# Sliding-window queries projected feature-major, in a two-layer hybrid decoder trunk

## The chip, the core and the metric

The kernel runs on one core of a Trainium2 chip. The profile knows five engines of that core: TensorE, shown as PE with its weight loads apart as PEld; VectorE (DVE), ScalarE (ACT), GpSimd (POOL), and SyncE (SP), whose queue issues all the kernel's DMAs. The metric is the time on the device in microseconds, lower is better. A profiled execution is one execution of the same program with the hardware profiler on; its span is the time from the first to the last instruction of the program.

## What is computed

A decoder trunk of two equal layers on 512 tokens of 1024 features, all in float32. One projection of the normalized input feeds two branches:

```python
h = rmsnorm(x, pre_mix_g)
proj = h @ w_in
(dn_q, dn_k, dn_v, dn_z, dn_b, dn_a, sw_q, sw_k, sw_v, gate_a, gate_b) = split(proj)
y_a = deltanet_branch(dn_q, dn_k, dn_v, dn_z, dn_b, dn_a, ...) @ w_up_dn
y_b = swa_sink_branch(sw_q, sw_k, sw_v, positions, sinks) @ w_up_sw
mix = (sigmoid(gate_a) * y_a + sigmoid(gate_b) * y_b) @ w_o
x = x + rmsnorm(mix, post_mix_g)
ff = square(relu(rmsnorm(x, pre_mlp_g) @ w_ff1)) @ w_ff2
x = x + rmsnorm(ff, post_mlp_g)
```

The second branch is what the change touches. It has 16 query heads of 64 features and 2 key/value heads (8 query heads share one), a window of 128 tokens and a learned sink for each head. The first 16 features of every query and key head are rotated: with halves x1 and x2 of 8 features each, `x1*cos - x2*sin` and `x2*cos + x1*sin`, angles by token position. The columns b and a of the projection (8 each) are the write strength and the decay of the first branch.

## The kernel before

**Number format.** Every large product is made from three matmuls: an operand is split into a rounded part (`_h`, a cast on ACT) and a rest (`_l`, a subtraction on DVE), and h·h, h·l and l·h are summed in PSUM. Weights come in pieces of at most 128x1024 (`load`, L265, five buffers `wr`) and are split by `prefetch` (L311: ACT L319, DVE L320) into four buffers each of `wh` and `wl`, so that conversion runs four pieces ahead of use.

**Two layouts.** `mm_a` (L331) takes a 128-column piece of weights as the stationary operand and streams 512 tokens: 24 matmuls of 512 columns, the result is [feature, token]. `mm_a2` (L340) is the same in two halves of 256 tokens. `mm_b` and `mm_b4` (L350, L373) keep 128 tokens stationary and stream weight columns: the result is [token, feature].

**The start of a layer.** The normalized input is transposed tile by tile (128 tokens each; `norm_turn`, L449, matmuls L455 into `ps_n`) into `hT`. The 1296 columns b, a, query, key, value are then projected in [token, feature] by three chunks of 432 columns (`NB`), each of 4 token tiles x 24 matmuls: chunk 0 at L495 to L559, chunks 1 and 2 at L655 to L659. `evac_b` (L590) copies them to `ba`, `qt[t]` (four tiles 128x1024) and `kv[t]`. In the first layer the work up to chunk 0 has an order on PE, ACT, DVE and SP that is written out by hand (`Order`); in the second layer the last tiles of the layer before and chunk 0 are in one such order on PE alone. Between chunk 0 and 1 stand the decay tables: a row `gd` is stored to DRAM, loaded back spread over 128 partitions (L646), masked on POOL (L647), exponentiated on ACT (L649, L651) and stored (`dd`).

**Attention.** Sixteen groups (tile t of 128 queries, key head g, e: even or odd heads of the eight), in the order t, g, e. `att_rope` (L770) rotates queries and keys of a tile on POOL; `att_prep` (L787) makes the values' two parts and transposes the keys (`ps_k`, L801); `att_q` (L810) transposes the queries of (t, g) by four PE transposes into `ps_q` (L814), and ACT L819 and DVE L820 scale and split them. Then a group makes its scores (L846, L847), a softmax on DVE and ACT (L850 to L870), a transpose of the probabilities (`ps_pt`, L876), and the product with the values (L892), written back over the queries in `qt[t]` as [feature, token] (L895, L896). At the end 32 pieces of 128x128 are split into `oT` for the up-projection (L1118 to L1124).

**What fills PE beside it.** `MIX` names for each of the 16 groups the projection units traced ahead of it: K (a DeltaNet key head, with its conv and its triangular matrix stored to DRAM), G and GA (merge gates). After the groups come the DeltaNet projections (`d_dense`), the up-projection, and the head-by-head chain.

**Order.** Everything outside the hand-written orders is placed by a list scheduler at build time: on each engine an instruction goes when its inputs are ready by a planner's model of durations, the earlier traced first. On the chip each queue then runs in that fixed order and waits where the plan was too early. SP's queue is one of those queues.

Of the kernel before, what the change touches and what calls it, by code (L numbers as in the profile page):

```python
# [20 lines left out]
P = 128  # L21
# [16 lines left out]
OFF_B, OFF_GA, OFF_GB = 4096, 5392, 6416  # L38
NB = 432
# [4 lines left out]
XB = 6  # L44

MIX = "G K K G K K G K K G K K G GA GA GA".split()
NA = sum(c.count("A") for c in MIX)
NA2 = NA + 2
LASTK = max(i for i, c in enumerate(MIX) if "K" in c)
PMB = 2  # L50


def chunk_order(depth):
# [3 lines left out]
    for l in range(depth):  # L57
        a_in = lambda w, c: out.append(("chunk", w, l, 0, c, 0))
        b_in = lambda w, r, c, n: out.append(("chunk", w, l, r, c, n))
        for n in range(3):  # L60
            for j in range(4):
                b_in("w_in", j * 256, OFF_B + n * NB, NB)
        n_ = {"K": 0, "G": 0, "A": 0}
        for c in "".join(MIX):
            a_in("w_in", {"K": OFF_K, "G": OFF_GB, "A": OFF_GA}[c] + n_[c] * P)
            n_[c] += 1
# [41 lines left out]
def pack(inputs, depth=2):  # L108

    keys = chunk_keys(depth)  # L110
    out = np.zeros((len(keys), P, 1024), np.float32)
    for i, (name, l, r, c, n) in enumerate(keys):
        k, n = (2, n) if n else (8, P)
        w = np.asarray(inputs[name])[l, r:r + k * P, c:c + n].reshape(k, P, n)
        out[i, :, :k * n] = w.transpose(1, 0, 2).reshape(P, k * n)
    return out
# [3 lines left out]
def hybrid_trunk(ctx, tc, x, positions, pre_mix_g, dn_conv_w, dn_a_log, dn_dt_bias, dn_norm_g,  # L120
# [35 lines left out]
    def X4(name):  # L156
        return up.tile([P, D], F32, name=name, tag="x4", bufs=XB)

# [87 lines left out]


    xd = dr.tile([S, D], F32, name="xd")
    gad = dr.tile([KT, P, 512], F32, name="gad")
# [15 lines left out]
    def load(key):  # L265

        wr = wp.tile([P, 1024], F32, name="wr", bufs=WR)
        w = 2 * key[4] if key[4] else 1024
        dma(wr[:, :w], wpk[index[key], :, :w])
        return wr  # L270

    def blocks(a, n_):
        return a[:, :2 * n_ if n_ else 1024].rearrange("p (k c) -> p k c", k=2 if n_ else 8)

    def seven(w, l, r0):
# [23 lines left out]
        return [(lambda f=f, j=j: f(j), 512) for f in makes for j in range(2)]  # L299
# [3 lines left out]
    for kind_, *key in chunk_order(depth):  # L303
        if kind_ == "seven":
            specs.extend(seven(*key))
        else:
            specs.append((tuple(key), key[4]))
# [3 lines left out]
    def prefetch(n, wr=None, sub=tt):  # L311
        while len(pre) < min(n, len(specs)):
# [5 lines left out]
            w = 2 * n_ if n_ else 1024  # L318
# [31 lines left out]
    def mm_b(ps, ws, aT, t, ks=range(KT)):  # L350
        tsl = slice(t * P, (t + 1) * P)
        for k in ks:
            hi, lo = aT[k]
            wh, wl = ws[k // 2]
            mm(ps, lhsT=hi[:, tsl], rhs=wh[:, k % 2, :], start=k == 0, stop=False)  # L355
            mm(ps, lhsT=hi[:, tsl], rhs=wl[:, k % 2, :], start=False, stop=False)  # L356
            mm(ps, lhsT=lo[:, tsl], rhs=wh[:, k % 2, :], start=False, stop=k == KT - 1)  # L357
# [54 lines left out]
    def gain(g):  # L412
        gb = X4("gb")
# [50 lines left out]
    def post_tile(a0g, ps1, add1, q0, gb, xsrc):  # L464
# [4 lines left out]
        xo = X4("xo")  # L469
# [12 lines left out]
    def pre_begin(l):  # L482
        if l > 0:
            return halves_of(gain(pre_mix_g[l])), *quads("h")

        row = X4("row")
        dma(row[0:1, :], pre_mix_g[l].rearrange("(o d) -> o d", o=1))
# [5 lines left out]
    for l in range(depth):  # L493

        pb0 = [b("ps_b") for b in (PM, PM, PK, PS)]  # L495
        nbs = slice(0, NB)
        if l == 0:
            order = Order(nc.tensor, nc.scalar, nc.vector, nc.sync)
            order.begin()
            xts = [X4("x0") for t in range(NT)]  # L500
# [10 lines left out]
            part = lambda t, j: mm_b(pb0[t][:, nbs], pre, hT, t, range(2 * j, 2 * j + 2))  # L511
# [16 lines left out]
            for j in range(2):  # L528
                part(1, j)
            xs.append(scale(2))  # L530
            ps2 = norm_turn(xs[2], 2, qs, 0)
            prefetch(3, wrs[2])
            for t in range(2):
                part(t, 2)
            rs.append(rstd("nr", *q[3]))
            xs.append(scale(3))
            norm_turn(xs[2], 2, qs, 1, ps2)
            ps3 = norm_turn(xs[3], 3, qs, 0)
            prefetch(4, wrs[3])
            for j in range(3):  # L540
                part(2, j)
            for t in range(3):
                part(t, 3)
# [822 lines left out]
```

## Time and profile before

| | |
|---|---|
| median of 3 timed runs | 1876.22 us (1875.23 to 1876.54) |
| profiled execution: time, span | 1874.57 us, 1872.9 us |
| instructions | 26807 |
| DVE, ACT, POOL busy | 68%, 50%, 11% of the span |
| moved by DMA | 255.40 MB, the queue of SP takes 42.0% of the 16 engines' time |

In the profile's rows a matmul row has a start, a modelled duration that overlaps the next one, and in brackets the idle time before it with what ended it. Since matmuls overlap, the cost of one is read from the distance between two starts. Names like `ps_q<-ident,qt` say what is written and read.

### The profile page before, as it was taken

The page shows a single profiled execution, that of the slowest core. Times are in us where ns is not written, and L with a number is a line of the kernel's source. Part 1 is how long each engine was busy: PE and PEld are TensorE (multiplying, and loading weights), DVE is VectorE, ACT ScalarE, POOL GpSimd, SP SyncE. Part 2 cuts the span into 40 slices and gives each one's busy share as a digit, 9 for nine tenths or more (in the row PEclk, how much of TensorE's full clock was granted, in tenths as well). Part 3 has the DMA queues.
Part 4 walks back from the last instruction along what each step waited for, and adds up shares of the span by engine and source line. Part 5 has one row for each costly group of instructions (what it writes and reads, how often), then busy time and mean ns, then how long its engine had stood idle before and what let it go on. Part 6 is the DMA issues. An engine that isn't in the chain of part 4 may idle for free. (4 is left out here: it accounts for less than half of the span.)

```text
span 1872.9 us, 26807 instructions
## 1 busy us (share of the span) xinstructions
PE 1847.6 (99%) x9716; PEld 1534.1 (82%) x9716; DVE 1281.5 (68%) x2466; ACT 939.7 (50%) x1913; POOL 208.1 (11%) x385
## 2 busy tenths in 40 slices
PE   8999999999999999999999999999999999999998
PEld 7888788888888888888888887888888888888886
DVE  5499795777656667684556997857775667586834
ACT  6678732344434645454356887233333346454442
POOL 1322102121100000000012221022111000000000
PEclk9999999999999999999999999999999999999999
DMA  5633436333363253544245333553433533534631
GB/s 179 202 115 117 120 125 196 102 119 109 86 215 127 91 188 97 176 168 170 83 143 188 103 126 105 160 173 102 125 97 110 194 124 99 183 114 158 205 119 45
DMA packets 123445, 255.40 MB, mean 136 GB/s; under 512 B 32609, under 2 KB 49313, under 8 KB 123314
## 3 DMA queue, kind: packets, MB, share of 16 engines
q1 hardware_dynamic: 123314, 253.71, 42.0%
q8 instruction: 76, 1.25, 0.3%
q14 instruction: 55, 0.45, 0.1%
HBM read 224.70 MB, written 28.97 MB: 135 GB/s over the span
## 5 line engine op out<-in xcount | busy, mean ns | idle before, releaser
L320 DVE TENSOR_TENSOR wl<-wr,wh 128x1024 fp32r<-128x1024 f32 (+1 forms) x332 | 402.6, 1222 | 331.2 <-ACT wh L319 323.4
L319 ACT CAST wh<-wr 128x1024 fp32r<-128x1024 f32 (+1 forms) x332 | 344.1, 1041 | 561.8 <-PE ps_f L336 145.9
L335 PE MATMUL ps_f<-g_h,wh 128*128 128x512 f32 x448 | 174.3, 389 | 0.0
L336 PE MATMUL ps_f<-g_l,wh 128*128 128x512 f32 x448 | 174.3, 389 | 0.0
L337 PE MATMUL ps_f<-g_h,wl 128*128 128x512 f32 x448 | 174.3, 389 | 0.0
L397 PE MATMUL ps_p<-wl,P_h 128*128 128x512 f32 x336 | 131.2, 391 | 0.8 <-DVE wl L320 0.8
L399 PE MATMUL ps_p<-wh,P_l 128*128 128x512 f32 x336 | 130.8, 389 | 0.0
L395 PE MATMUL ps_p<-wh,P_h 128*128 128x512 f32 x336 | 129.5, 389 | 0.0
L434 POOL TENSOR_TENSOR pr<-pq,pw 128x1 f32<-128x1 f32 x16 | 9.3, 583 | 809.5 <-DVE pq L433 809.5
L336 PEld LDWEIGHTS ps_f<-g_l,wh 128*128 128x128 f32 x448 | 84.1, 188 | 17.5
L335 PEld LDWEIGHTS ps_f<-g_h,wh 128*128 128x128 f32 x448 | 84.1, 188 | 17.4
L337 PEld LDWEIGHTS ps_f<-g_h,wl 128*128 128x128 f32 x448 | 84.1, 188 | 17.4
L397 PEld LDWEIGHTS ps_p<-wl,P_h 128*128 128x128 f32 x336 | 63.1, 188 | 15.6 <-DVE wl L320 2.3
L395 PEld LDWEIGHTS ps_p<-wh,P_h 128*128 128x128 f32 x336 | 63.1, 188 | 13.3 <-ACT wh L319 0.2
L399 PEld LDWEIGHTS ps_p<-wh,P_l 128*128 128x128 f32 x336 | 63.1, 188 | 12.8
L382 PE MATMUL ps_b<-wh,h_h 128*128 128x432 f32 (+1 forms) x192 | 71.1, 371 | 0.0
L383 PE MATMUL ps_b<-wl,h_h 128*128 128x432 f32 (+1 forms) x192 | 70.4, 367 | 0.0
L384 PE MATMUL ps_b<-wh,h_l 128*128 128x432 f32 (+1 forms) x192 | 70.0, 366 | 0.0
L285 DVE TENSOR_TENSOR wr<-wr 128x1024 f32<-128x1024 f32 x48 | 58.0, 1221 | 2.4 <-DMA wr<-in_weights_dram 1.9
L335 PE MATMUL ps_qp<-h_h,wh 128*128 128x512 f32 x128 | 54.9, 429 | 0.0
L336 PE MATMUL ps_qp<-h_l,wh 128*128 128x512 f32 x128 | 54.1, 423 | 0.0
L864 ACT ACTIVATE M<-M,nm 128x128 f32<-128x128 f32 x128 | 49.8, 391 | 5.9 <-DVE nm L859 5.9
(356 smaller groups left out, 4855.4 us busy)
## 6 DMA issues: line engine op xcount, KB each, us to landing
wr<-in_weights_dram SPq DMA_DIRECT2D x308, 512.0 KB
wr<-in_weights_dram SPq DMA_DIRECT2D x24, 432.0 KB
D<-dd SPq DMA_DIRECT2D x32, 256.0 KB
xd<-xo SPq DMA_DIRECT2D x12, 512.0 KB
xt<-xd SPq DMA_DIRECT2D x24, 256.0 KB
D<-gd SPq DMA_DIRECT2D x16, 256.0 KB
dd<-D SPq DMA_DIRECT2D x16, 256.0 KB
kkd<-kk SPq DMA_DIRECT2D x16, 256.0 KB
```

The costliest lines, as they stand in the source:

```text
L285: tt(out=a, in0=a, in1=o, op=ALU.add)
L319: nc.scalar.copy(wh[:, :w], wr[:, :w])
L320: sub(out=wl[:, :w], in0=wr[:, :w], in1=wh[:, :w].bitcast(F32), op=ALU.subtract)
L335: mm(ps, lhsT=wh[:, k, :], rhs=hi, start=k == 0, stop=False)
L336: mm(ps, lhsT=wh[:, k, :], rhs=lo, start=False, stop=False)
L337: mm(ps, lhsT=wl[:, k, :], rhs=hi, start=False, stop=k == KT - 1)
L382: mm(pss[t], lhsT=hi[:, tsl], rhs=wh[:, r, :], start=k == 0, stop=False)
L383: mm(pss[t], lhsT=hi[:, tsl], rhs=wl[:, r, :], start=False, stop=False)
L384: mm(pss[t], lhsT=lo[:, tsl], rhs=wh[:, r, :], start=False, stop=k == KT - 1)
L395: mm(pss[t], lhsT=hi[:, c], rhs=wh[:, r, :], start=first, stop=False, skip_group_check=onto)
L397: mm(pss[t], lhsT=hi[:, c], rhs=wl[:, r, :], start=False, stop=False, skip_group_check=onto)
L399: mm(pss[t], lhsT=lo[:, c], rhs=wh[:, r, :], start=False, stop=last, skip_group_check=onto)
```

## The change

Only keys, values, b and a stay in [token, feature]: `NB` becomes 272, and the weights of these columns are packed in three pieces of three, three and two 128-row blocks (`w_bkv`, `rows_of`). The queries become eight units of `mm_a`, called `q_unit`, whose result stands in two tiles `q8[g]` of 128x2048 as [feature, token]; unit 0 is made in the hand-written order by `mm_a2`. Four units are traced before the attention, four among its first three groups (`MIX`).

Rotation of the queries now goes through DRAM and DVE: `q_rope` stores the rows to be rotated from four places of `q8[g]` (8 partitions each), loads them packed into 128 partitions, once as they are and once with the halves exchanged, makes three DVE operations with tables `cosT` and `sinT`, stores the result and loads it back to the four places. The tables are made once in `rotary` (16 ACT copies, 8 PE transposes), which is traced later than before, and loaded in each layer. The transposes of `att_q` fall away: it reads `q8` directly. Groups run in the order (0,0), (1,0), (0,1), (1,1), (2,0), (2,1), (3,0), (3,1) for (t, g), and `att_ready` issues rotation and transposition of keys and the splitting of queries one group ahead; values (`att_values`) are prepared inside the group. The decay tables are traced after the third query unit (`decays`). `X4` buffers of 128x1024 become halves of `X8` buffers of 128x2048, three in all.

```diff
-OFF_B, OFF_GA, OFF_GB = 4096, 5392, 6416
-NB = 432
+OFF_B, OFF_SQ, OFF_SK, OFF_GA, OFF_GB = 4096, 4112, 5136, 5392, 6416
+NB = 272
...
-MIX = "G K K G K K G K K G K K G GA GA GA".split()
+MIX = "QQ KQ QK G KG KG G KG K GK GK G A A A A".split()
 NA = sum(c.count("A") for c in MIX)
-NA2 = NA + 2
+NA2 = NA + 1
+BKV = 0, 3, 6
...
+        for c in range(2):
+            ct = T[6 + c]("ct")
+            cv = ct.rearrange("p (t a b i) -> p t a b i", t=NT, a=2, i=HALF)
+            for a in range(2):
+                for t in range(NT):
+                    src = cs[:, t, c, :].unsqueeze(1).broadcast_to([P, 8, HALF])
+                    act(out=cv[:, t, a], in_=src, func=AF.Copy, scale=-1.0 if c > a else 1.0)
+            ps = PS("ps_cs")
+            for t in range(NT):
+                tr(ps[:, t * P:(t + 1) * P], ct[:, t * P:(t + 1) * P], ident)
+            ctT = T[6 + c]("ctT")
+            nc.scalar.copy(ctT, ps)
+            dma(csd[c], ctT)
...
-            ws = [weights() for _ in range(4)]
-            for t in range(NT):
-                mm_b(pb0[t][:, nbs], ws, hT, t, range(4))
-                if t == 1:
-                    norm_turn(xs_next[2], 2, nxt[1])
-                mm_b(pb0[t][:, nbs], ws, hT, t, range(4, KT))
-                if t == 1:
-                    norm_turn(xs_next[3], 3, nxt[1])
+            ws = [weights() for _ in range(3)]
+            pb0 = [PZ("ps_b"), PZ("ps_b"), None, None]
+            for t in range(2):
+                mm_b(pb0[t][:, :NB], ws, hT, t, rows=3)
+            ps_q0, w_q0 = PM("ps_q"), weights()
+            for j in range(2):
+                mm_a2(ps_q0, hT, 0, w_q0, range(j * 4, j * 4 + 4))
+                norm_turn(xs_next[2 + j], 2 + j, nxt[1])
+            for t in range(2, 4):
+                pb0[t] = (PM, PK)[t - 2]("ps_b")
+                mm_b(pb0[t][:, :NB], ws, hT, t, rows=3)
+            mm_a2(ps_q0, hT, 1, w_q0)
...
+        def q_rope(g):
+            spots = [(q8[g][e * HD + a * HALF:e * HD + (a + 1) * HALF].rearrange("p (m n) -> p m n", m=4),
+                      lambda d, a=a, e=e: d[g, a].rearrange("(m e) i n -> e i m n", e=2)[e])
+                     for e in range(2) for a in range(2)]
+            for a, d in spots:
+                dma(d(qd), a)
+            r_, rs_ = T[2]("rq"), T[3]("rq")
+            flat = lambda d: d.rearrange("a b i n -> (a b i) n")
+            dma(r_, flat(qd[g]))
+            for a in range(2):
+                dma(rs_[a * 64:(a + 1) * 64], qd[g, 1 - a].rearrange("b i n -> (b i) n"))
+            tt(out=r_, in0=r_, in1=tables[0], op=ALU.mult)
+            tt(out=rs_, in0=rs_, in1=tables[1], op=ALU.mult)
+            tt(out=r_, in0=r_, in1=rs_, op=ALU.add)
+            dma(flat(qrd[g]), r_)
+            for a, d in spots:
+                dma(a, d(qrd))
+
+        def q_unit(m):
+            if m == 0:
+                ps = ps_q0
+            else:
+                ps = PM("ps_q")
+                mm_a(ps, hT)
+            nc.scalar.copy(q8[m // 4][:, m % 4 * 512:(m % 4 + 1) * 512], ps)
+            if m % 4 == 3:
+                q_rope(m // 4)
...
         def att_q(t, g):
-            ps = PS("ps_q")
-            for i in range(4):
-                j = g * 4 + i
-                tr(ps[:, i * P:(i + 1) * P], qt[t][:, j * P:(j + 1) * P], ident)
+            q_ = c4(q8[g])[:, :, t * P:(t + 1) * P]
...
+        for m in range(4):
+            q_unit(m)
+            if m == 1 and l == 0:
+                rotary()
+            if m == 2:
+                tables = q_tables()
+                decays()
+        def att_ready(i):
+            if i + 1 < 16 and groups[i + 1][1:] == (0, 0):
+                att_rope(groups[i + 1][0])
+            if i < 16:
+                t, g, e = groups[i]
+                if (g, e) == (0, 0):
+                    att_keys(t)
+                if e == 0:
+                    att_q(t, g)
+        att_rope(0)
+        att_ready(0)
         for i in range(16):
...
             late = g
+            att_ready(i + 1)
             if i > LASTK:
                 steps(3)
...
-        for t in range(NT):
-            tsl = slice(t * P, (t + 1) * P)
-            for g in range(2):
-                for j in range(g * 4, g * 4 + 4):
-                    hi, lo = oT[j]
-                    split(qt[t][:, j * P:(j + 1) * P], hi[:, tsl], lo[:, tsl])
+        for j in range(KT):
+            split(q8[j // 4][:, j % 4 * 512:(j % 4 + 1) * 512], *oT[j])
```

In the first layer the hand-written order at the start changes with it: tile 1 gets three of its eight row blocks ahead of the transposes of tile 2 and not four, `evac_b` of tiles 0 and 1 stands inside that order, and after the transposes of tile 3 the first half of query unit 0 comes ahead of tile 3's projection, the second half behind it.

## What is predicted, and why

> **What bounds the kernel now.** I read the page's busy times first, then busy time by stage, then PE's waits, then PE's own rows.
>
> ```profile
> span 1872.9 us, 26807 instructions
> PE 1847.6 (99%) x9716; PEld 1534.1 (82%) x9716; DVE 1281.5 (68%) x2466; ACT 939.7 (50%) x1913; POOL 208.1 (11%) x385
> core 0: us, PE busy (x) PEld busy (x) DVE busy (x) ACT busy (x) POOL busy (x), PEclk, DMA share, GB/s
> 0.00:76.00 76.00, 68.85 (x335) 62.58 (x336) 36.71 (x92) 49.15 (x111) 15.00 (x36) 1.00 0.66 214
> 76.00:230.00 154.00, 151.26 (x788) 123.59 (x787) 129.00 (x374) 116.72 (x340) 36.38 (x68) 1.00 0.36 112
> 941.00:1004.00 63.00, 60.34 (x315) 56.60 (x314) 31.11 (x65) 38.10 (x91) 12.04 (x21) 1.00 0.58 195
> 1004.00:1158.00 154.00, 151.26 (x789) 123.61 (x788) 128.94 (x375) 116.62 (x340) 36.75 (x70) 1.00 0.36 112
> ```
>
> PE is the bound: of 1872.9 us it lacks 25.3. The four windows are the stages that the change rebuilds, in both layers: the start of a layer (0 to 76, 941 to 1004) and the sixteen attention groups (76 to 230, 1004 to 1158). There PE lacks 7.2, 2.7, 2.7 and 2.7 us, 15.3 together: no better order can give back more than that. What else can be won is work of PE's own. Work of DVE, ACT or POOL counts only where PE waits for it:
>
> ```profile
> PE ps_n L455 <- DVE xs L446: 5.5, 7, 2.2
> PE ps_pt L876 <- ACT M L870: 3.9, 6, 0.8
> ...
> PE ps_g L627 <- DVE lw L625: 1.0, 1, 1.0
> ```
>
> In the attention it waits mainly for the softmax on ACT (3.9 us, six times in both layers); no row says that it waits for queries or keys.
>
> **Step 1: query transposes go.** They are 64 matmuls, in 16 bursts of four.
>
> ```profile
> L814 PE MATMUL ps_q<-ident,qt 128*128 128x128 f32 x64 | 9.6, 272 | 0.0
> 79.88 0.28 PE L801 MATMUL ps_k<-ident,kv 128*128 128x128 f32 x1
> 79.99 0.60 PE L814 MATMUL ps_q<-ident,qt 128*128 128x128 f32 x4
> 80.34 0.48 PE L335 MATMUL ps_kp<-h_h,wh 128*128 128x512 f32 x1
> ...
> 131.64 0.60 PE L814 MATMUL ps_q<-ident,qt 128*128 128x128 f32 x4
> 132.00 0.48 PE L337 MATMUL ps_kp<-h_h,wl 128*128 128x512 f32 x1
> 132.31 0.39 PE L335 MATMUL ps_kp<-h_h,wh 128*128 128x512 f32 x1
> ```
>
> Matmuls overlap, so the cost is the distance between starts: 79.99 to 80.34 and 131.64 to 132.00, 0.355 us a burst, 5.7 for 16. Behind a burst the next matmul takes 0.31 and not 0.23 (step 2): 0.08 more. Half of the bursts belong to groups that transpose keys as well (79.88), which stays, so this counts 8 times: 0.6. **Sum: -6.3 us.** Nothing fills the place, as PE has other units ready in almost all of these 308 us.
>
> **Step 2: the same columns, cut otherwise.** A layer projected 4 x 24 x 3 = 288 matmuls of 432 columns. Now it is 96 of 272, 7 units x 24 of 512, and 48 of 256 (unit 0): 124416 columns in both.
>
> ```profile
> 59.90 0.36 PE L382 MATMUL ps_b<-wh,h_h 128*128 128x432 f32 x1
> ...
> 74.22 0.35 PE L384 MATMUL ps_b<-wh,h_l 128*128 128x432 f32 x1
> 74.41 0.39 PE L335 MATMUL ps_gb<-h_h,wh 128*128 128x512 f32 x1
> ...
> 79.64 0.40 PE L337 MATMUL ps_gb<-h_h,wl 128*128 128x512 f32 x1
> ...
> 600.94 0.28 PE L346 MATMUL ps_f<-g_h,wh 128*128 128x256 f32 x1
> ...
> 608.01 0.28 PE L348 MATMUL ps_f<-g_h,wl 128*128 128x256 f32 x1
> ```
>
> 75, 24 and 60 matmuls from the first to the last of each pair: 14.32/74 = 0.1935 us, 5.23/23 = 0.2274, 7.07/59 = 0.1198. No row has 272 columns; it lies between 0.1198 and 0.1935, and a straight line gives 0.1265. Before 288 x 0.1935 = 55.73 us; after 96 x 0.1265 + 168 x 0.2274 + 48 x 0.1198 = 56.09. **+0.36 a layer, +0.7.** If 272 columns cost no more than 256 it is -0.3 a layer.
>
> **Step 3: tables.** Eight transposes in the first layer, 8 x 0.355/4 and twice 0.08 behind them: **+0.9**. Their 16 ACT copies and the sine now stand behind the second query unit. PE runs a fixed order, so if the plan puts the transposes too early it waits: `ps_g` above, also behind a chain of small ACT and DVE operations, cost 1.0. I take 0 and keep 2 as the upper bound, as three more query units are there to fill.
>
> **Step 4: the two starts.** In the first layer, when the transposes of tile 3 begin, 36 matmuls of 432 are done (7.0 us); now 57 of 272 would be (7.2 us). The weights for the next unit come free earlier, as only the last piece is held to the end. I take 0, between -1 and +1. In the second layer the transposes of tiles 2 and 3 wait for a DVE and ACT chain that the change doesn't touch:
>
> ```profile
> 952.53 0.35 PE L357 MATMUL ps_b<-wh,h_l 128*128 128x432 f32 x1
> 954.61 1.29 PE L455 MATMUL ps_n<-ident,xs 128*128 128x128 f32 x8 [1.73 <-DVE xs L446]
> 955.66 0.44 PE L355 MATMUL ps_b<-wh,h_h 128*128 128x432 f32 x1
> ```
>
> Until 955.66 PE got 48 matmuls of 432 done, 9.3 us of work. Now its order holds 48 of 272 and 24 of 256 ahead of that point, 6.1 + 2.9 = 8.9 us: **+0.3**, and the idle time of 1.73 us grows to some 2.7.
>
> The trace has a second fact for this place. At the start of the kernel, after PE had waited for its input:
>
> ```profile
> 13.72 0.71 PE L355 MATMUL ps_b<-wh,h_h 128*128 128x432 f32 x1
> ...
> 16.02 0.48 PE L355 MATMUL ps_b<-wh,h_h 128*128 128x432 f32 x1
> 16.34 0.36 PE L356 MATMUL ps_b<-wl,h_h 128*128 128x432 f32 x1
> 16.54 0.36 PE L357 MATMUL ps_b<-wh,h_l 128*128 128x432 f32 x1
> ```
>
> From 13.72 to 16.02 lie six distances, 0.38 us on average; from 16.34 on it is 0.20, while the wait of 1.73 us at 954.61 leaves it at 0.19 to 0.20. So a long pause makes PE slow for a while, and a short one doesn't. [...]
>
> **Step 5: rotation by DRAM, the one new wait.** Query unit 3's result goes out by four stores, comes in by three loads, three DVE operations, one store, four loads, and only then ACT and DVE can split the queries of group 0. The nearest chain in the trace is the decay row: stored, and loaded back.
>
> ```profile
> 43.08 0.33 SPq L639 DMA_DIRECT2D gd<-gT  x1
> 43.51 0.37 SPq L642 DMA_DIRECT2D egd<-egT  x1
> 44.50 2.71 SPq L646 DMA_DIRECT2D D<-gd  x6
> ...
> 47.73 0.64 POOL L647 TENSOR_SCALAR_AFFINE_SELECT D<-D 128x512 f32<-128x512 f32 x1 [28.97 <-DMA D<-gd]
> ...
>   POOL D L647: 2.9, 2
> L820 DVE SCALAR_TENSOR_TENSOR qT<-ps_q,qT 64x512 fp32r<-64x512 f32 x32 | 22.0, 689 | 1.8 <-ACT qT L819 0.9
> L819 ACT ACTIVATE qT<-ps_q 64x512 fp32r<-64x512 f32 x32 | 18.9, 591 | 6.8 <-DVE qT L820 5.2 <-PE ps_q L814 1.3
> L595 ACT COPY qt<-ps_b 128x432 f32<-128x432 f32 x8 | 3.7, 510 | 0.0
> ```
>
> A store takes 1.4 us from its issue to that of the load behind it, a load 3.2 to its user, each further issue on SP 2.71/6 = 0.45. The chain: copy 0.5; stores 1.4 + 3 x 0.45 = 2.8; loads 3.2 + 2 x 0.45 = 4.1; DVE 3 x 0.69 = 2.1; store 1.4; loads 3.2 + 1.4 = 4.6; splitting 0.6 + 0.7. That is **16.8 us**. In that time PE has query units 4 and 5, 48 x 0.2274 = 10.9 us, and behind them a K unit of 5.5 us that needs nothing of the chain: 16.4 together. So PE is covered if its fixed order puts the K unit ahead of the first scores, and waits 16.8 - 10.9 = 5.9 us a layer if it does not. Between 0 and 11.8 for both layers; I take 0, since in the decay chain the plan was late for ACT only (2.9 us before L649 in both layers, the row "POOL D L647") and PE lost nothing by it. Queued behind the waiting instructions: on ACT the copies of units 4 and 5 and the weight casts (four converted pieces lie ahead, 4 x 5.5 = 22 us), on DVE the other half of the conversion, on SP the weight loads, which also run at least four pieces ahead. The chain for units 4 to 7 has groups 2 and 3 and more units ahead of its user and is not late.
>
> **Costed at nothing**, since PE doesn't wait for it: POOL's query rotation goes; DVE gains six rotation operations a layer (4.1 us) and loses by splitting `oT` in 8 pieces and not 32, and by the copies of `kv`:
>
> ```profile
> L407 DVE TENSOR_TENSOR oT_l<-qt,oT_h 128x128 fp32r<-128x128 f32 x64 | 16.7, 298 | 4.9 <-ACT qq L665 2.9 <-ACT oT_h L406 1.5 <-PE ps_k L801 0.5
> L598 DVE COPY kv<-ps_b 128x256 f32<-128x256 f32 x8 | 3.3, 416 | 0.0
> ```
>
> That is 32 x 0.30 - 8 x 0.69 + 4 x 0.42 = 5.8 us a layer off DVE, so its 129 us in the attention's 154 don't grow. One gate unit more stands in the attention and one less behind the up-projection: same work of PE.
>
> **The sum:** -6.3 + 0.7 + 0.9 + 0.3 = **-4.4 us**. The profiled execution took 1874.57 (span 1872.9 and 1.7 around it), which would become 1870.2. The median of the runs is 1876.22, 1.65 above it; the same 4.4 off gives **1871.8 us**.
>
> **The rivals.** A measurement of this kernel tells 0.2% (3.75 us) from no change, so 1872.5 and 1880.0 are the limits.
>
> *The rotation isn't covered* (the other side): PE's order has the first scores right behind unit 5, and PE waits up to 5.9 us a layer: 1871.8 + 11.8 = 1883.6. From 2.2 us a layer the gain is gone, from 4.1 the kernel is slower by 0.2%. For it: the chain is four DMA trips long, and the plan was already late by 1.4 us a layer in a chain of two. Against it: the scheduler knows that DMAs take time and has a K unit at hand. Chance 0.33: 0.13 of it within 0.2%, 0.20 slower.
>
> *The attention's own waits go too*: with `ps_q` gone the three `ps` buffers serve only keys, probabilities and outputs, and queries and keys are ready a group early. At most the 2 x 2.7 us that PE lacks there: 1871.8 - 5.5 = 1866.3. Against it: those waits are for softmax on ACT. Chance 0.15.
>
> [...] Chance 0.05, within 0.2%.
>
> *The forecast*: 0.47, between 1869.5 and 1874; 0.33 of it faster by over 0.2%, 0.14 within.
>
> Faster 0.33 + 0.15 = 0.48; within 0.14 + 0.13 + 0.05 = 0.32; slower 0.20. The range leaves out the lowest part of the second rival and the upper part of the first: 1866 to 1881.
>
> **What would show it.** PE's rows: no L814; 272-column starts 0.126 apart; a pause of about 2.7 us before the last `ps_n` of the second layer's start. For the rotation: PE's idle time before the first `ps_s` of each layer, and idle ACT, DVE and SP released by the DMAs of `rq` and `q8`. I am wrong if that idle time is over 2 us, if PE lacks more in the attention than 2.7 us a layer, or if the starts of 272 columns lie nearer to 0.19.

## The result, and the profile after

The changed kernel takes **1899.97 us** (median of 4 runs, 1898.65 to 1900.26) against 1875.72 (1874.81 to 1876.54) for the kernel before in the same series: ratio 1.0128, 95% interval 1.011 to 1.0146. It is 1.3% slower; the forecast was 1871.8 and its range ended at 1881.

The page of the changed kernel, its first lines and the granted TensorE clock in 40 slices:

```profile
span 1898.2 us, 26679 instructions
...
PE 1855.4 (98%) x9708; PEld 1526.3 (80%) x9708; DVE 1285.4 (68%) x2420; ACT 942.6 (50%) x1882; POOL 183.4 (10%) x337
...
PEclk9989999999999999999999999999999999999999
```

PE is still the bound, yet it is busy 7.8 us longer than before (1847.6), though the work given to it is less. Of its waits the first three rows matter (line, what it waited for, total, times, longest):

```profile
PE ps_pt L934 <- ACT M L926: 7.5, 9, 3.0
PE ps_n L489 <- DVE xs L480: 5.8, 5, 3.4
PE ps_us L370 <- DVE tmp L819: 5.4, 2, 2.7
...
PE ps_kp L370 <- ACT q L725: 1.3, 1, 1.3
```

The transposes of the probabilities wait twice as long for the softmax as before (3.9), and the first matmul of the up-projection, which waited for nothing, waits 2.7 us in each layer. To place the loss I took the distances between neighbouring matmul starts and subtracted from each the distance that undisturbed matmuls of its width have in these traces (0.2267 us for 512 columns, 0.1927 for 432, 0.1265 for 272, 0.1183 for 256, 0.090 for 128). What is left, in us, I call pauses; it holds waits and slow matmuls alike. A layer's start is counted from the first transpose of its input (`ps_n`). The level of the last row depends on what is subtracted for matmuls of 64 and 32 columns; only its differences are read.

| pauses | layer 1 before | after | layer 2 before | after |
|---|---|---|---|---|
| start of the layer to the first scores | 7.4 | 9.4 | 5.8 | 7.8 |
| attention, from the first scores | 13.1 | 25.4 | 13.1 | 17.2 |
| 14 us around the first `ps_us` | 0.0 | 4.5 | 0.0 | 4.5 |
| from there to the first `ps_ud` | 18.7 | 18.5 | 18.7 | 18.4 |

The sum grows by 28.9. By the counts of matmuls the work falls by 4.2 (up to the first `ps_us`, a layer had 288 x 0.1927 + 32 x 0.090 and has 96 x 0.1265 + 48 x 0.1183 + 168 x 0.2267, with 8 x 0.090 for the tables in the first). That leaves 24.7 of the 25.3 by which the span grew. So by these counts the work was saved as forecast, and seven times as much came as pauses.

Layer 1 of after by stage:

```profile
core 0: us, PE busy (x) PEld busy (x) DVE busy (x) ACT busy (x) POOL busy (x), PEclk, DMA share, GB/s
0.00:101.70 101.70, 92.16 (x466) 77.08 (x467) 45.30 (x104) 59.18 (x140) 13.32 (x40) 1.00 0.58 188
101.70:130.00 28.30, 22.24 (x100) 17.76 (x99) 22.86 (x70) 19.56 (x58) 2.04 (x2) 0.76 0.24 75
130.00:258.00 128.00, 124.52 (x623) 98.93 (x622) 106.83 (x305) 99.85 (x284) 25.52 (x40) 1.00 0.44 137
258.00:271.00 13.00, 10.24 (x44) 7.68 (x42) 12.44 (x20) 7.59 (x13) 3.04 (x3) 1.00 0.32 110
```

In the 28 us behind the first scores PE issues 100 matmuls, its clock is granted at 0.76, and DVE is busy 81%; from 258 to 271 DVE is busy 96% and PE 79%. These are the two places at which to look.

### The profile page after: what moved, and what is told of

Same layout as the page of the kernel before. It is cut to its first block, busy times and chain, and to the rows that moved or that the text cites. A ratio compares the mean times of both kernels' runs of the same rounds, so it can differ in the third digit from the quotient of the medians.

```text
span 1898.2 us, 26679 instructions
## 1 busy us (share of the span) xinstructions
PE 1855.4 (98%) x9708; PEld 1526.3 (80%) x9708; DVE 1285.4 (68%) x2420; ACT 942.6 (50%) x1882; POOL 183.4 (10%) x337
## 4 chain that ended last, share of the span: by engine, by line
PE 79%; ACT 8%; DVE 6%; issue 4%; DMA 2%; POOL 1%; SPq 0%; POOLq 0%; DVEq 0%; ACTq 0%
PE ps_f L370 5%; PE ps_f L371 5%; PE ps_f L372 5%; PE ps_p L432 4%; PE ps_p L434 4%; PE ps_p L430 4%; PE ps_us L370 2%; PE ps_us L371 2%; PE ps_us L372 2%; PE ps_qp L370 2%; PE ps_b L419 2%; PE ps_b L417 2%; PE ps_b L418 2%; ACT M L926 1%; PE ps_vp L371 1%
## 5 line engine op out<-in xcount | busy, mean ns | idle before, releaser
L370 PEld LDWEIGHTS ps_f<-g_h,wh 128*128 128x128 f32 x448 | 84.1, 188 | 17.2
L432 PEld LDWEIGHTS ps_p<-wl,P_h 128*128 128x128 f32 x336 | 63.1, 188 | 15.3 <-DVE wl L355 2.1
L370 PE MATMUL ps_us<-oT_h,wh 128*128 128x512 f32 x128 | 51.5, 402 | 5.4 <-DVE tmp L819 5.4
L370 PE MATMUL ps_kp<-h_h,wh 128*128 128x512 f32 x128 | 50.4, 394 | 2.5 <-ACT q L725 1.3
L372 PE MATMUL ps_qp<-h_h,wl 128*128 128x512 f32 x128 | 52.6, 411 | 0.0
```

Source lines behind the costliest of these rows:

```text
L370: mm(ps, lhsT=wh[:, k, :], rhs=hi, start=k == 0, stop=False)
L372: mm(ps, lhsT=wl[:, k, :], rhs=hi, start=False, stop=k == KT - 1)
L432: mm(pss[t], lhsT=hi[:, c], rhs=wl[:, r, :], start=False, stop=False, skip_group_check=onto)
```

## The experiments

Theories, as the expectations name them: **A** the rotation's chain of transfers, **B** the preparation one group ahead, **C** `oT` split in 8 large pieces, **D** the list of units beside the groups, **E** (found on the way) GpSimd's mask held up by VectorE. All times are medians; ratios are to the kernel before in the same series, with 95% intervals.

| run | us | ratio | interval |
|---|---|---|---|
| after | 1899.97 | 1.0128 | 1.0110 to 1.0146 |
| e1 no rotation | 1893.20 | 1.0096 | 1.0081 to 1.0111 |
| e2 decays early | 1897.81 | 1.0123 | 1.0108 to 1.0138 |
| e3 decays late | 1901.42 | 1.0138 | 1.0121 to 1.0155 |
| e4 split in 32 pieces | 1896.11 | 1.0118 | 1.0101 to 1.0135 |
| e5 own group | 1898.70 | 1.0124 | 1.0107 to 1.0141 |
| e6 no rotation, old list and order | 1883.46 | 1.0038 | 1.0025 to 1.0051 |
| e7 e6, own group, 32 pieces | 1880.55 | 1.0027 | 1.0018 to 1.0037 |
| e8 e7 with rotation | 1908.16 | 1.0172 | 1.0157 to 1.0187 |
| e9 before, transposes twice | 1888.33 | 1.0066 | 1.0051 to 1.0081 |
| e10 e6 in the new order | 1891.75 | 1.0083 | 1.0068 to 1.0098 |
| e11 rotation on GpSimd's queue | 1892.93 | 1.0089 | 1.0072 to 1.0106 |
| e12 more units | 1903.36 | 1.0155 | 1.0134 to 1.0177 |
| e13 e7, no mask | 1875.61 | 0.9996 | 0.9986 to 1.0005 |
| e14 e10, no mask | 1880.57 | 1.0017 | 1.0007 to 1.0026 |
| e15 e11 and e4 | 1888.19 | 1.0058 | 1.0043 to 1.0073 |
| e16 before, no mask | 1874.44 | 0.9985 | 0.9976 to 0.9994 |
| e17 after, no mask | 1896.16 | 1.0114 | 1.0097 to 1.0131 |
| e18 e15, no mask | 1883.50 | 1.0043 | 1.0028 to 1.0058 |

A difference of two ratios times 1876 gives us; by the intervals such a difference is good to ±2.5 us (e13 against e7) up to ±4.6 us (e11 against after). In e13 to e18 the runs of before have medians of 1876.4 to 1877.4, in the others 1875.0 to 1875.7, so ratios compare better than medians. Each edit is planned anew by the list scheduler, so a run can also move instructions that it doesn't name: e11 changes only who issues some transfers, and the orders of PE, ACT and DVE all differ from those of after.

### The rotation's chain (e1, e2, e3, e11)

```diff
-            if m % 4 == 3:
-                q_rope(m // 4)
```

> The changed kernel without the rotation of the queries (no trips through DRAM, no DVE operations for it; the output is without that rotation). Theory A (the chain): the rotation's chain took 46 us from the end of query unit 3 (55.3) to the first scores (101.7), six units were used up meanwhile, and the attention then starts with too little beside it; without the chain the first scores come at 65 to 80 us and the attention's extra waits (about 10 us in the first layer, 8 in the second) go: 1880 to 1884 us. Theory B (one group ahead): preparing the next queries and keys on ACT and DVE stands in front of the softmax of the current group; then the waits stay without the chain: 1893 us or more.

Measured 1893.2: 6.0 us less by the ratio, at the edge of theory B's case. Pauses in the attention of layer 1 fall from 25.4 to 19.2; in layer 2 they are 18.3 against 17.2, and the wait before the up-projection stays. As the main cause theory A falls; as a part of some 6 us it holds.

e2 and e3 move one call, `decays()`: in e2 ahead of the first query unit, in e3 behind the fourth.

> The decay tables are traced ahead of the query units, as the kernel before had them early, and not behind the third. Theory A with its part A1 (the tables' 16 rows of exponentials on ACT and their stores on SP lengthen the chain): the first scores come some 10 us earlier and time falls by 5 to 12 us, to 1888 to 1895. If the chain is long by its own trips and by SP's order alone, the first scores move by less than 4 us and time stays within 3 us of 1900.

> The decay tables are traced behind the fourth query unit and its rotation. A1: as with the early tables, 1888 to 1895, if the planner now lets the rotation's transfers and copies go first. If it gives nothing to the chain, or the tables then come late for the first K unit, 1897 to 1903.

Neither differs from after by more than its interval; in e2 the first scores come at 100.9 us instead of 101.7. So the decays on ScalarE alone don't make the chain long. Its stations in after, from the timeline (start, length, engine; SPq is SyncE's queue): first SyncE,

```profile
61.20 0.35 SPq L706 DMA_DIRECT2D qd<-q  x1
63.06 3.56 SPq L689 DMA_DIRECT2D dd<-D  x3
66.67 1.39 SPq L706 DMA_DIRECT2D qd<-q  x3
70.34 0.51 SPq L711 DMA_DIRECT2D rq<-qd  x1
...
85.09 0.29 SPq L706 DMA_DIRECT2D qd<-q  x1
85.48 0.33 SPq L715 DMA_DIRECT2D qrd<-rq  x1
...
88.61 1.31 SPq L717 DMA_DIRECT2D q<-qrd  x4
```

then VectorE, and ScalarE at both ends:

```profile
74.39 2.32 DVE L736 SCALAR_TENSOR_TENSOR kk<-ps_kp,cw,kk 128x509 f32<-128x509 f32 x3 [3.27 <-issue]
...
78.07 0.69 DVE L712 TENSOR_TENSOR rq<-rq,cosT 128x512 f32<-128x512 f32 x1
80.61 1.23 DVE L355 TENSOR_TENSOR wl<-wr,wh 128x1024 fp32r<-128x1024 f32 x1 [1.85 <-ACT wh L354]
81.75 0.68 DVE L713 TENSOR_TENSOR rq<-rq,sinT 128x512 f32<-128x512 f32 x1
```

```profile
57.60 0.56 ACT L725 COPY q<-ps_q 128x512 f32<-128x512 f32 x1
...
96.27 0.60 ACT L785 ACTIVATE sgb<-ps_gb 128x512 f32<-128x512 f32 x1 [2.52 <-PE ps_gb L372]
96.76 0.62 ACT L883 ACTIVATE qT<-q 64x512 fp32r<-64x512 f32 x1
```

From the copy at 57.60 to the split at 96.76 it takes 39 us, where the forecast had 15.5. Most of the difference is standing in line. Three of the four stores stand on SyncE's fixed queue behind three decay stores (66.67); the rotation on VectorE stands behind the conv of a K unit and a weight conversion (78.07 to 83.2); its store stands at 85.48 directly behind a store of the *next* half, which had to wait for the copy of unit 7 at 84.48; and the split stands behind a gate unit that ScalarE waits for.

```diff
             for a, d in spots:
-                dma(d(qd), a)
+                nc.gpsimd.dma_start(d(qd), a)
...
```

(and so for every transfer of `q_rope`)

> After, with the transfers of the query rotation issued by GpSimd instead of SyncE, so that they stand behind none of the decay stores and behind no wait of the other half. Theory A (the length of the chain makes the loss, and SyncE's queue makes some 10 to 15 of its 46 us): first scores in layer 1 at 85 to 92 instead of 101.7, time 1891 to 1897. Rival (queue is not what holds it; the copies and the adds on ScalarE and VectorE are): first scores at 98 or later, 1897 to 1902.

Measured 1892.93, 7.3 us less than after by the ratio, within the intervals as much as leaving the rotation out. The first scores come at 94.3 in layer 1, 7 us earlier but later than theory A expected (85 to 92), as VectorE and ScalarE still hold the chain. The 36 us behind the first scores of layer 1, after and then e11:

```profile
101.70:137.70 36.00, 28.94 (x130) 22.61 (x128) 28.70 (x84) 25.35 (x77) 4.31 (x4) 0.81 0.26 81
```

```profile
94.00:130.00 36.00, 32.98 (x167) 26.23 (x168) 33.08 (x89) 27.13 (x80) 9.01 (x14) 1.00 0.41 128
```

PE's clock is back at 1.00 and PE gets 37 matmuls more done. What SyncE's queue stood at in after, from 84 to 132 us, shows in its own waits:

```profile
SPq L715 <- DVE rq L714: 21.7, 1, 21.7
```

This is the store of the *second* half's rotated queries. From 98.6 to 120.4 us SyncE issues nothing, no weights either. The loss goes with this stand and not with the length of the chain: in layer 2 the chain is about as long (44.1 us from the end of unit 3 to the first scores, 46.4 in layer 1), but there no transfer of SyncE stands longer than 13.9 us, and the first 20 us behind the scores have 2.9 us of pauses. In layer 1 they have 10.8, in before 3.0 and 2.7, in e11 3.1 and 2.9. In e11 the second half's store comes hardly earlier (118.3), but it stands on GpSimd's queue. How the stand reaches PE is not shown: e11 has another order on ScalarE too, which splits the next weights 9 us behind the first scores (103.6) where after does so 19 us behind them (120.3).

So the run with another issuing engine is 7.3 us faster, and what stood in SyncE's queue in after was not issue time (0.32 us for this store, at 120.37) but the transfer's wait of 21.7 us for its data.

### The bulk split of `oT` (e4, e15)

```diff
-        for j in range(KT):
-            split(q8[j // 4][:, j % 4 * 512:(j % 4 + 1) * 512], *oT[j])
+        for t, g in ((0, 0), (1, 0), (0, 1), (1, 1), (2, 0), (2, 1), (3, 0), (3, 1)):
+            for j in range(g * 4, g * 4 + 4):
+                hi, lo = oT[j]
+                tsl = slice(t * P, (t + 1) * P)
+                split(q8[g][:, j % 4 * 512 + t * P:j % 4 * 512 + (t + 1) * P], hi[:, tsl], lo[:, tsl])
```

> The parts of the attention's output are made in 32 pieces of 128x128, one tile and head pair at a time, in the order in which the groups end, and not in 8 pieces of 128x512 at the end. Theory C: the bulk of five pieces on DVE stands in front of the V projection's convolution, so that its PSUM buffer comes free late and PE waits 2.8 us before the up-projection in each layer, with a slower clock behind it (1.6): 1891 to 1895 us. If that wait comes from the late end of the attention alone, it stays: 1898 to 1902.

> After with the rotation's transfers issued by GpSimd (e11, -7.0) and oT split in 32 pieces (e4, -3.9). If the two costs are separate: 1888 to 1891. If they share a cause: 1891 to 1894. Below 1881 in no theory.

e4 is 1.9 us below after by the ratio, which is inside the interval of such a difference, and 3.1 by the medians' distances from before; it lands between its two cases. e15 is 5.8 below e11. In both the pauses around the first `ps_us` fall to 1.5 a layer (from 4.5 in after, 5.9 in e11). VectorE and then PE in after show why:

```profile
265.58 2.48 DVE L442 TENSOR_TENSOR oT_l<-q,oT_h 128x512 fp32r<-128x512 f32 x4
268.28 0.73 DVE L736 SCALAR_TENSOR_TENSOR vv<-ps_vp,cw,vv 128x509 f32<-128x509 f32 x1
...
270.26 0.73 DVE L736 SCALAR_TENSOR_TENSOR vv<-ps_vp,cw,vv 128x511 f32<-128x511 f32 x1
```

```profile
268.08 0.39 PE L372 MATMUL ps_zp<-h_h,wl 128*128 128x512 f32 x1
271.14 0.77 PE L370 MATMUL ps_us<-oT_h,wh 128*128 128x512 f32 x1 [2.66 <-DVE tmp L819]
271.70 0.63 PE L371 MATMUL ps_us<-oT_l,wh 128*128 128x512 f32 x1
...
274.26 0.49 PE L371 MATMUL ps_us<-oT_l,wh 128*128 128x512 f32 x1
274.59 0.40 PE L372 MATMUL ps_us<-oT_h,wl 128*128 128x512 f32 x1
```

A piece over all four token tiles can't be split before the last group of its head is done, so the splits pile up at the end, ahead of the conv `vv`, whose third operation (270.26 to 270.99) frees the PSUM buffer that `ps_us` needs; the wait names `tmp`, VectorE's next instruction. In 32 pieces most were split long before. The expected 5 to 9 us came only in part in e4, and as 5.8 with the queue mended (13.1 us for both). By e15's cases the costs don't share a cause.

### List, order, one group ahead (e5, e6, e7, e8, e10, e12)

e5 calls the preparation of keys, queries and values at the start of their own group, as before.

> After, with keys, queries and values of the attention prepared at the start of their own group as in before, not one group ahead; all else as after (1900.0). Theory B (the work done one group ahead stands before the softmax of the running group on ScalarE and VectorE, and this is most of what the attention still lacked without the rotation: 19.2 and 18.3 us of pauses against 13.1 in before): 1888 to 1892. Rival D (the units: the planner has put units ahead of the first scores, or the new list gives the groups too little cover; where the preparation stands matters little): 1897 to 1901.

No difference. Theory B falls.

```diff
-MIX = "QQ KQ QK G KG KG G KG K GK GK G A A A A".split()
+MIX = "G K K G K K G K K G K K G GA GA GA".split()
...
-        for m in range(4):
+        for m in range(8):
             q_unit(m)
```

e6 has this, `NA2` as before, no `q_rope`, and the groups in the order t, g, e. e7 adds e5's edit and 32 pieces, e8 puts `q_rope` back into e7, e10 is e6 in the groups' order of after.

> No query rotation (left out, as in e1), and all eight query units ahead of the attention with before's list of K, G and A units and before's order of the groups; keys and queries still one group ahead, oT still in 8 pieces. Theory D (the list of units and the order of the groups set the attention's pauses): attention pauses back from 19 to about 13 us a layer, 1880 to 1884 against 1893.2 of e1. Theory B: 1891 to 1895.

> As e6 (no query rotation, all eight query units first, before's list of units; 1883.5), but with the order of the groups of after. If the list of units made the 9.8 us between e1 and e6: 1882 to 1886. If the order of the groups made it: 1890 to 1893.

e6 is 10.9 us below e1, with pauses of 16.5 a layer in the attention. That looked like theory D, but e10 shows that the list is innocent: with pauses of 20.9 and 20.5 in the attention it stays 8.4 us above e6, and hardly below e1. **The order of the groups costs 8 us** (8.4 ± 3.7) without the rotation.

> As e6, and also keys, queries and values prepared in their own group and oT split in 32 pieces in the order of the groups: what is left of the change is the projection of the queries as feature by token, the narrower b/a/k/v and the two starts. If the price of the change lies in the attention's order and in the bulk split, this is 1870 to 1876 (before 1875, less the 4.4 us of work that the forecast counted, plus up to 3 at the starts). If it lies in the new columns and starts themselves, 1880 or more.

> As e7 but with the query rotation through DRAM kept. Theory A (the chain of some 46 us costs what no unit covers; after the fourth unit there are four query units, 22 us, and whatever K and G units the planner takes): e7 plus 5 to 10 us, 1877 to 1886. If the planner covers it with units and the attention doesn't miss them: within 2 us of e7.

e7 comes out at the edge of its second case, at 1.0027, but not for that case's reason. Little but the projection by feature is left of the change, its matmuls are 4.2 us less, and it still loses 5 us, most of it because the attention has 16.0 and 16.4 us of pauses instead of 13.1. e8 is 27 us above e7 where 5 to 10 were expected. With no query units left for the time between, PE stands 4.5 us before the first scores of layer 1; in layer 2 it stands 4.4 us for a weight conversion, 19 us behind its first scores:

```profile
PE ps_s L902 <- DVE qT L884: 5.1, 2, 4.5
PE ps_kp L372 <- DVE wl L355: 4.4, 1, 4.4
```

That the price of the same chain is only 6 to 7 us in after speaks for the query units among its groups, though e8 differs from after in the order and the pieces too.

e12 puts two more A units into e4's list (`"QQ KQ QK GA KG KG GA ..."`, `NA2 = NA`); one unit fewer is then left behind the last head, and the last step of that head's normalization is left out with it.

> After with oT split in 32 pieces (e4, 1896.1) and six A units in the attention's list instead of four, two of them in its first half; they are taken from later stages. Theory D (the units that cover the chain are missing later beside the groups; the pauses, and the lower clock behind the longer ones, come from that): 1888 to 1893. Rival (the groups wait for ScalarE and VectorE whatever TensorE has; two more tanh make it no better): 1895 to 1899.

Pauses in the attention are 24.7 and 19.1 against 26.3 and 17.8 in e4, and 2 to 3 us a layer more later on. e12 is 6.9 us above e4, outside both cases. More work for PE doesn't help; theory D falls.

### What a transpose costs, and the mask on GpSimd (e9, e13, e14, e16, e17, e18)

```diff
-                tr(ps[:, i * P:(i + 1) * P], qt[t][:, j * P:(j + 1) * P], ident)
+                for _ in range(2):
+                    tr(ps[:, i * P:(i + 1) * P], qt[t][:, j * P:(j + 1) * P], ident)
```

> The kernel before, with each of its 64 query transposes of the attention issued twice into the same place (same result, twice the work on TensorE). The forecast of Step 1 took such a transpose at full price since TensorE was busy 98% of the attention: then this is 1875.7 plus 5.8 to 6.3, 1881 to 1882. Rival (the attention's length is set by the chains of its groups on ScalarE, VectorE and GpSimd as well, so that 2.9 us a layer more or less on TensorE goes into waits): 1875 to 1878.

Both cases miss: 64 transposes more cost 12.4 us by the ratio. By the stages each layer's attention grows by 5.8, of which 2.9 is the matmuls and 2.7 to 3.0 pauses. It looks as if PE's work and the groups' chains on the other engines were so tightly fitted that a shift either way makes pauses: in e7, which differs from before in more than this, the same 2.9 us are taken out, and 3 us of pauses come.

One place where such pauses come from shows in e10, in the rows of POOL and VectorE:

```profile
195.84 0.63 POOL L942 TENSOR_SCALAR_AFFINE_SELECT pc<-pf_h 128x512 fp32r<-128x512 f32 x1
...
198.90 2.35 DVE L355 TENSOR_TENSOR wl<-wr,wh 128x1024 fp32r<-128x1024 f32 x2
198.98 2.79 POOL L942 TENSOR_SCALAR_AFFINE_SELECT pc<-pf_l 128x512 fp32r<-128x512 f32 x1 [2.51 <-DVE es L915]
```

```profile
201.82 0.50 PE L948 MATMUL ps_o<-pc,vp 128*128 128x512 f32 x1 [1.89 <-POOL pc L942]
```

The same mask takes 0.63 us or 2.79, the latter as long as two weight conversions run on VectorE beside it. Sorted by what VectorE runs when a mask starts: under instructions that read PSUM, or only one tensor in SBUF, nearly all take 0.64. Under `wl<-wr,wh` they take 1.59 on average in after (4 masks), 1.63 in e7 (4), 2.05 in e10 (4); under `kk<-th,kk` up to 1.1 in before, 1.0 in after and 2.2 in e10; under the split of the queries, `qT<-ps_q,qT`, 0.64 in before (8), and under the new `qT<-q,qT`, which reads two tensors in SBUF, 0.93 to 1.15 (7 in after, e7 and e10). The mask of 198.98 ends at 201.77, 0.5 us behind the two conversions (201.25). What in the two engines makes it so is not shown.

```diff
-                    b = T[6]("pc", F32R)
-                    nc.gpsimd.affine_select(out=c4(b), in_=c4(a), pattern=[[0, 4], [1, P]],
-                                            compare_op=ALU.is_ge, fill=0.0, base=0,
-                                            channel_multiplier=-1)
-                    pvs.append((at["v", t], 256, b))
+                    pvs.append((at["v", t], 256, a))
```

> e7 without GpSimd's mask of the attention weights (the weights go unmasked into the second product; matmuls the same). Theory E (GpSimd's mask is held up by VectorE's instructions with two SBUF inputs, and ps_o waits for it: 3.7 us by e7's waits, and what follows from them): 1875 to 1877.5 against 1880.6. Rival (the pauses come from the shorter list of TensorE work before each group and show up elsewhere): 1879 to 1881.

> e10 without the mask. Theory E (the order of the groups costs 8.2 us since it puts the masks beside VectorE's two-input instructions; ps_o waits 3.8 us a layer for pc in e10, 0.7 in e6): 1883 to 1886 against 1891.8. Rival (the order costs by something else): 1888 to 1892.

> The kernel before without the mask, as the measure for e13 and e14. Theory E: TensorE waits 0.4 us for pc in before, so 1874 to 1876. If the mask holds up the groups in before as well, 1870 to 1873, and e13 shows nothing of the change.

e13 falls by 5.8 us against e7, inside theory E's case, e14 by 12.4 against e10, below both its cases, and before by 2.8 (e16). So the mask costs these kernels more than it costs before: net of e16 it makes 3.0 us of e7's time and 9.6 of e10's, more than the order had cost (e6 without the mask was not run). The runs leave out the whole mask, its own 0.64 us included; that the delay under VectorE makes the difference is read from the rows above.

> After without GpSimd's mask. In e13 and e14 taking it out was worth 5 and 11 us, in before 1 to 3. TensorE waits for the mask in after for 1.3 us only, so by the waits alone 1897 to 1899; if the delay also sits in the chains of the groups, as in e14, 1889 to 1894.

> e15 (transfers of the rotation by GpSimd, oT in 32 pieces; 1888.2) without the mask. If the three causes are all: within 3 us of e14 and of before without the mask, 1877 to 1882. If half of the query units among the groups has a price of its own: 1884 or more.

In after itself the mask is worth only 2.6 us (e17, between its two cases), no more than in before, and 2.8 in e15. So nothing shows it to be a cause of the 24 us as the kernel stands, though intervals of over ±4 us leave room for a part. e18 falls between its two cases and is still 10.9 us above e16, with pauses of 16.6 and 15.4 in the attention (e16: 12.4 and 12.4). Its waits are small and spread, for the softmax (3.9), `pf_h` (2.1) and `qT` (1.8).

**What is shown, then:** of the 24 us of loss, 7.3 go when the rotation's transfers leave SyncE's queue and another 2 to 6 when the split is made in small pieces, together 13.1 (e15, ± 4.4). **What stays open** are the other 11, and the 4 us of saved work that don't show. Most of it lies in the attention, where e15 still has 19.0 and 17.5 us of pauses, 10 more than before. The order of the groups and the tight fit of the attention are the candidates (8.4 us in e10, 6.2 us of pauses in e7's attention, both measured without the rotation); no run undoes the order with the rotation in place. No version that computes everything beat the kernel before.

## Why the prediction was wrong, step by step

Two terms that it put at nothing failed by measure: Step 5, the rotation's chain (7.3 us in e11), and VectorE's load (2 to 6 us in e4 and e15). The cause of the other 11 us stays open; Step 1's premise fails with them.

**Step 1, transposes go, -6.3.** The matmuls are gone from the trace. The step's "nothing fills the place, as PE has other units ready" failed: e7 has the saving and 3 us a layer of new pauses (with other differences), and e9 shows that 2.9 us of such work moves the attention of before by 5.8.

**Step 2, same columns, +0.7.** Right. 272 columns:

```profile
30.23 0.29 PE L390 MATMUL ps_b<-wh,h_h 128*128 128x272 f32 x1
...
33.00 0.28 PE L391 MATMUL ps_b<-wl,h_h 128*128 128x272 f32 x1
```

22 distances in 2.77 us, 0.126 each, as interpolated.

**Step 3, tables, +0.9.** Inside its bound: the wait that was taken as 0 came as 0.9 us, for the copies of `ct`, where the bound was 2. In return the 1.0 us that `ps_g` waited in before is gone.

**Step 4, the starts, 0 and +0.3.** Too small: the pauses ahead of the scores grow by 2.0 in each layer. More than half is a wait that no step has: one matmul in each layer waits 1.3 us until ScalarE, busy with the decay tables, has copied a query unit out of PSUM (`ps_kp` at 67.83, `ps_q` at 1005.81). In the second layer, the pause that was to reach some 2.7 us (the lines quoted for it give 1.73 + 0.3 = 2.0) came as 1.76 and 0.54, and the matmuls behind it were slow all the same:

```profile
969.97 0.63 PE L489 MATMUL ps_n<-ident,xs 128*128 128x128 f32 x4 [1.76 <-DVE xs L480]
971.14 1.11 PE L489 MATMUL ps_n<-ident,xs 128*128 128x128 f32 x4 [0.54 <-DVE h_l L495]
...
972.28 0.43 PE L391 MATMUL ps_b<-wl,h_h 128*128 128x272 f32 x1
972.51 0.43 PE L392 MATMUL ps_b<-wh,h_l 128*128 128x272 f32 x1
```

0.23 apart and not 0.126, at a granted clock of 0.50 (970.78 to 974.20). In the sum of the chances, 0.05 stands for a pause past a limit at which PE gets slow. No run shows such a limit: slow matmuls came behind 1.76 us here, while before has 1.73 us and matmuls 0.19 to 0.20 apart behind it. The last section has what the traces show of the granted clock.

**Step 5, the rotation's chain, taken as 0.** This step was mis-sized, and the wait stood elsewhere. The stores, loads and operations were added up as if the queues were empty: 16.8 us. From the end of unit 3 (55.3) to the first scores (101.7) it is 46.4, by what stands *ahead* on SyncE, VectorE and ScalarE. But this length was covered: idle time before the first scores, the sign that the step named, is 0 in both layers, as the plan had put units there (the 0.8 us that `ps_s` waits for `qT` is before the second group, at 108.38). What failed is what the step said of the queue *behind* the chain, the weight loads that "run at least four pieces ahead", and of the second half, whose chain "is not late": its store holds SyncE's queue for 21.7 us, and the 20 us behind the first scores of layer 1 have 10.8 us of pauses where before has 3.0. The rival "the rotation isn't covered" has a fair price (up to 11.8; e1 gives 6.0, e11 7.3), by luck, as its wait isn't the one that came. Of the three signs of being wrong, one came: PE lacks 12.3 and 8.1 us in the two attentions, and not 2.7.

**Costed at nothing, DVE's load.** VectorE does get fewer instructions for `oT` (16 of 0.69 us instead of 64 of 0.30), but *when* they run was not looked at. Most of them stand behind the last groups, and 3 of the 4.5 us a layer around `ps_us` come from them (e4). This term has no rival in the prediction and is the plainest miss.

**The bound "PE lacks 15.3 us in these stages"** was read as all that order could give back. Whether it bounds the gains no run shows: the count of pauses puts 13.1 us a layer into the attention of before where busy time lacks 2.7, as modelled durations overlap. It said nothing about losses: the range left no room for a worse fit of the attention, though the rows quoted there have DVE busy 129 and ACT 117 of 154 us.

## What to carry to other kernels

Add up a new chain of transfers with what stands ahead of it on each fixed queue, and ask what stands behind each of its waits: in after a store that waited 21.7 us for its data held up all that was to be issued after it on the same queue. Give the chain an issuing engine whose queue has little else to do (7.3 us in e11). Large pieces instead of small ones save instructions but come ready only with the last of their parts, so ask what is then late behind them (here PE, by 2.7 us a layer before `ps_us`). In a stage like this attention, with PE busy 151, DVE 129 and ACT 117 of 154 us, work taken off one engine is not a gain until the others' chains are shown to follow.

## What the runs showed of the hardware

The prediction took from the trace of before that a long pause makes PE slow and a short one, of 1.73 us, doesn't. In after the granted clock fell to half, 0.50, behind pauses of 0.9 us (at 110.62), 2.7 (at 271.05), 1.8 (at 970.78) and 2.7 (at 1206.30). The two of 2.7 us, before `ps_us`, were each followed by 3.4 us at half rate (0.43 us a matmul instead of 0.23, rows above), 1.5 us lost each time, while e2 has the same pauses of 2.7 us and no slow matmul behind them. Behind the first scores of layer 1 the clock was down before PE had idled longer than 0.9 us at a time, and it stayed at 0.50 from 110.62 to 124.28 as the waits went on. By the granted clock, after lost 0.7% of its span (13 us, not all of it while PE had work), before 0.1%.

The times of the changes show more. In the trace of after the granted clock changes only at whole multiples of 3.413 us from its first change: it falls at 110.62, 271.05, 970.78 and 1206.30 (0, 47, 252 and 321 of them) and is back at 124.28, 274.46, 974.20 and 1209.71 (4, 48, 253 and 322). Cut at such times, four stretches of after and then two of e2:

```profile
107.21:110.62 3.41, 1.75 (x13) 1.25 (x11) 2.47 (x6) 3.36 (x12) 0.00 (x0) 1.00 0.00 0
110.62:114.04 3.42, 3.10 (x9) 1.45 (x7) 2.83 (x11) 2.56 (x8) 0.00 (x0) 0.50 0.00 0
267.64:271.05 3.41, 0.83 (x4) 0.37 (x2) 3.41 (x8) 1.54 (x2) 0.00 (x0) 1.00 0.48 183
271.05:274.46 3.41, 3.32 (x8) 2.71 (x9) 3.41 (x15) 0.63 (x1) 0.00 (x0) 0.50 0.02 5
```

```profile
265.88:269.29 3.41, 1.69 (x8) 1.07 (x6) 3.41 (x8) 1.54 (x2) 0.00 (x0) 1.00 0.68 228
269.29:272.70 3.41, 2.41 (x11) 2.01 (x12) 3.41 (x12) 0.63 (x1) 0.00 (x0) 1.00 0.02 5
```

After's pause of 2.7 us lies inside one stretch, in which PE is busy 0.83 of 3.41 us, and the next stretch is slow. E2's pause lies across a border, and neither of its two stretches is followed by a slow one. Ahead of the end, the clock of after fell four times, behind stretches in which PE was busy 1.75, 0.83, 1.47 and 0.95 of 3.41 us. In before, a stretch with 1.69 of 3.42 us (951.53 to 954.95, the one with the pause of 1.73 us) left it at 1.00. So PE's busy time as the profile models it gives no sharp limit in these traces. A wait of 2.7 us on PE was followed by 1.5 us more of loss in after and by none in e2, and behind two waits of 0.8 and 0.9 us the clock of after stood at 0.50 for 13.7 us, in which PE waited another 3.0 and 1.3 us.
